# A hybrid decoder layer: the decay products of a group's heads in two blocks of four in place of four blocks of two

## The chip, the cores and the metric

One core of a Trainium2 chip runs the whole layer. The metric is the device time of one execution in microseconds (us), the median over runs.

The engines are named as the profile names them: PE is TensorE (PE for matmuls, PEld for its weight loads), DVE is VectorE, ACT is ScalarE, POOL is GpSimd, SP issues the loads of the weights.

## The reference

256 tokens go through one decoder layer of width 2048: a state-space branch and an attention branch in parallel, a gated merge, and a feed-forward part. The change lies in the state-space branch, which has 8 groups of 8 heads; all 256 positions are one chunk:

```
xbc = silu(causal_dwconv(xbc, conv_w, conv_b))          # after xbc, z = h @ w_in
a_cs = cumsum(dt * A)                                   # per head
decay = exp(where(causal, a_cs[l] - a_cs[s], -inf))     # per head, 256 x 256
cb = einsum('bclgn,bcsgn->bclsg', C, B)                 # per group
y_diag = einsum('bclsg,bclsgr,bcsgrp->bclgrp', cb, decay, x * dt)
y = y_diag + x * d_skip
yg = rmsnorm_per_group(y * silu(z)) * norm_w
```

The result is multiplied by `w_ssm_out`. All arithmetic is to be accurate to single precision.

## The kernel before

**Weights.** The kernel streams every weight matrix once, in pieces of 128 x 2048 (`unit`). A piece comes in two chunks. Each chunk of 128 x 1024 is split into a rounded part `whi` (ACT, line 182) and a rest `wlo` (DVE, line 183), and PE multiplies it in 24 matmuls: 16 with `whi` (lines 214 and 215), then 8 with `wlo` (line 217). `whi` and `wlo` have three buffers each, so that a chunk's split can begin when PE is done with the chunk three before it. One piece is called a unit here.

**The state-space branch.** Step g of a loop runs the ten units of group g (`group_units`, numbered 0 to 9). Units 4 to 9 are each followed by a causal convolution: one instruction of ACT (line 752), then three of DVE (line 755). Then, in steps 1 to 7, come four more units (gates or parts of the output product); step 8 has only such units.

**The core of a group** (`core_steps`) is spread over the units of the next step. It is a list of steps, and after each unit `sp.tick()` emits the next one. For group 7 the list is one shorter and is given 10 ticks, so the first three ticks take two steps each. An empty list is a tick without work. The steps that matter here, for a pair p of heads (four pairs in a group):

- `dec(p)` makes the decay times `cb` for two heads: on ACT lines 820 to 823, on DVE line 824, then a copy `mhl` in two parts, line 828 on ACT and 829 on DVE. `mhl` has two buffers.
- `ydot(p)` is four matmuls on PE (lines 839 and 840, twice each), from `mhl` into two tiles `cc`, of which there are four. DVE then adds them up with six instructions on 64 partitions each: lines 842, 844 and 845 for either head. After pairs 1 and 3 a product with the gate follows (line 847).
- `norm1` starts the norm of the group with two squares on ACT (lines 852 and 853).

The four matmuls of a `ydot` stand on PE between the last matmul of one unit and the first of the next; such a run of lines 839 and 840 is called a block.

**Order.** On PE the order is that of the code. On DVE and ACT a scheduler sets the order of the instructions when the kernel is built, from its own costs; on the chip each engine then takes its instructions in that order.

Of the kernel before, what the change touches and what calls it, by code (L numbers as in the profile page):

```python
# [160 lines left out]
def _body(tc, nc, d, out):  # L161
# [45 lines left out]
    def c_tile():  # L207
        return psum.tile([128, 512], F32, name="cc", bufs=4)
# [46 lines left out]
    def sm(name, i=0, n=1, rows=slice(0, 128)):  # L255
        o, _ = _SMALL[name]
        return small[rows, o + i:o + i + n]
# [403 lines left out]
    for o in range(KT):  # L661
# [8 lines left out]
        g = gl.pop(o)  # L670
# [88 lines left out]
    def core_steps(g):  # L759
        pr = pre[g % 2]  # L760
        st = {}
        steps = []
# [25 lines left out]
        def xtr(s):  # L788
            def f():
                ps = c_tile()  # L790
                for i in range(4):
                    PE.transpose(ps[:, i * 128:(i + 1) * 128], pr[:, 4 + i, s * 128:(s + 1) * 128], ident)  # L792
                xf = sd.tile([128, 8, 64], F32, name="xf", bufs=2)
                dtc = acol[:, s, 64 + 8 * g:72 + 8 * g]
                V.tensor_tensor(xf, ps.rearrange("p (h c) -> p h c", c=64),
                                dtc[:, :, None].to_broadcast([128, 8, 64]), op=MUL)
                xff = xf.rearrange("p (a b) c -> p a b c", b=2)
                hi, lo = st["x"][:, s, :, 0:4:3], st["x"][:, s, :, 1:3]
                S.activation(hi, xff, AF.Copy)
                V.tensor_tensor(lo, xff, hi.bitcast(F32), op=SUB)  # L800
            return f

        def load_a(p):
            ab = sd.tile([128, 2, T], F32, name="ab", bufs=2)
            h0 = 8 * g + 2 * p
            nc.gpsimd.dma_start(ab, bass.AP(tensor=acs.tensor, offset=acs.offset + h0 * T,
                                            ap=[[0, 128], [T, 2], [1, T]]))
            st["ab", p] = ab

        def dec(p):  # L810
            def f():
                if p == 0:
                    load_a(0)
                if p < 3:
                    load_a(p + 1)
                ab = st.pop(("ab", p))
                h0 = 8 * g + 2 * p
                m = sd.tile([128, 2, 384], F32, name="m", bufs=2)
                for h in range(2):
                    S.activation(m[:, h, 0:256], ab[:, h], AF.Relu, scale=-1.0, bias=acol[:, 0, h0 + h:h0 + h + 1])  # L820
                    S.activation(m[:, h, 256:384], ab[:, h, 128:256], AF.Relu, scale=-1.0,
                                 bias=acol[:, 1, h0 + h:h0 + h + 1])
                S.activation(m, m, AF.Exp, scale=-1.0)
                V.tensor_tensor(m, m, st["cb"][:, None].to_broadcast([128, 2, 384]), op=MUL)
                if g == 0 and p == 0:
                    sd.tile([128, 16], F32, name="pad2")
                mhl = sd.tile([128, 2, 2, 384], F32R, name="mhl", bufs=2)
                S.activation(mhl[:, 0], m, AF.Copy)
                V.tensor_tensor(mhl[:, 1], m, mhl[:, 0].bitcast(F32), op=SUB)
                st["m", p] = mhl  # L830
            return f

        def ydot(p):
            def f():
                m = st.pop(("m", p))
                for h in range(2):
                    ps = c_tile().rearrange("p (a t) -> p a t", t=T)
                    x0, x1 = [st["x"][:, s, p, 2 * h:2 * h + 2].rearrange("p a c -> p (a c)") for s in range(2)]
                    PE.matmul(ps, x0, m[:, :, h, 0:256], start=True, stop=False)  # L839
                    PE.matmul(ps[:, :, 128:], x1, m[:, :, h, 256:384], start=False, stop=True)  # L840
                    rs, ls = slice(h * 64, (h + 1) * 64), slice(64 - h * 64, 128 - h * 64)
                    V.scalar_tensor_tensor(yz[rs, p], pr[rs, 4 + p], sm("ssm_d", 4 * g + p, 1, rs), ps[rs, 0],
                                           op0=MUL, op1=ADD)
                    V.tensor_tensor(yz[rs, p], ps[rs, 1], yz[rs, p], op=ADD)
                    V.tensor_tensor(yz[rs, p], ps[ls, 0], yz[rs, p], op=ADD)
                if p % 2:
                    V.tensor_tensor(yz[:, p - 1:p + 1], yz[:, p - 1:p + 1], pr[:, p - 1:p + 1], op=MUL)
            return f
# [15 lines left out]
        def norm2():  # L864
            r = st["r"]
            for i in range(4):
# [4 lines left out]
            S.activation(yh, yz, AF.Copy)  # L871
            V.tensor_tensor(yt[:, b, 1, o:o + 4], yz, yh.bitcast(F32), op=SUB)

        steps = [[dt_cols, silu] if g == 0 else silu, [xtr(0), xtr(1), bc], dec(0), dec(1), ydot(0), dec(2), ydot(1), dec(3), ydot(2), [ydot(3), norm1],
                 [], [], norm1b, norm2]

        if g == G - 1:
# [33 lines left out]
    for step in range(9):  # L911
        if step < 8:
            for i in group_units(step):
                sp.tick()
        outs = [(((step - 3) // 2), ((step - 3) % 2) * 4 + u) for u in range(4)] if step >= 3 else []
        ng = {1: 4, 2: 4, 8: 8}.get(step, 0)
        for _ in range(ng):
            gate_ssm(go)
            go += 1
            sp.tick()  # L920
        for q, u in outs:
            out_unit(q, u, acc_done(q))
            sp.tick()
        sp.flush()
        if step < 8:
            nu = 14
            if step == 7:
                nu = 10
            sp.add(core_steps(step), nu)
# [140 lines left out]
```

## Time and profile before

| | |
|---|---|
| median of 3 runs | 2020.08 us (2019.61 to 2021.86) |
| the profiled execution | 2020.08 us, its span 2018.3 us |
| PE busy | 2012.8 us (100% of the span), 17203 matmuls |
| DVE, ACT, POOL busy | 1496.2, 1189.3, 79.0 us (74%, 59%, 4%) |
| granted clock of TensorE | 1.0 of full speed in the mean |
| DMA | 402.40 MB, mean 199 GB/s |

The span is the time from the first to the last instruction of the core; 1.8 us of the execution lie outside. A busy share is a mean over the whole span. The trace gives start and duration of each instruction; matmuls overlap, so what one costs is read from the distance between two starts.

### The profile page before, as it was taken

The page shows a single profiled execution, that of the slowest core. Times are in us where ns is not written, and L with a number is a line of the kernel's source. Part 1 is how long each engine was busy: PE and PEld are TensorE (multiplying, and loading weights), DVE is VectorE, ACT ScalarE, POOL GpSimd, SP SyncE. Part 2 cuts the span into 40 slices and gives each one's busy share as a digit, 9 for nine tenths or more (in the row PEclk, how much of TensorE's full clock was granted, in tenths as well). Part 3 has the DMA queues.
Part 4 walks back from the last instruction along what each step waited for, and adds up shares of the span by engine and source line. Part 5 has one row for each costly group of instructions (what it writes and reads, how often), then busy time and mean ns, then how long its engine had stood idle before and what let it go on. Part 6 is the DMA issues. An engine that isn't in the chain of part 4 may idle for free.

```text
span 2018.3 us, 40758 instructions
## 1 busy us (share of the span) xinstructions
PE 2012.8 (100%) x17203; PEld 1988.8 (99%) x17203; DVE 1496.2 (74%) x2206; ACT 1189.3 (59%) x1640; POOL 79.0 (4%) x100
## 2 busy tenths in 40 slices
PE   9999999999999999999999999999999999999999
PEld 7999999999999999999999999999999999999999
DVE  7588877656788798888989886677777765677554
ACT  6466655544768867667677645565555553455333
POOL 0012210000000000000000000000000000000000
PEclk9999999999999999999999999999999999999999
DMA  7555555656556556555565575555555555555555
GB/s 290 188 182 182 181 182 205 234 204 213 185 193 220 202 201 209 193 193 193 195 209 178 196 274 202 191 190 196 200 189 190 201 195 188 194 201 190 190 185 169
DMA packets 64351, 402.40 MB, mean 199 GB/s; under 512 B 7655, under 2 KB 10264, under 8 KB 20648
## 3 DMA queue, kind: packets, MB, share of 16 engines
q1 hardware_dynamic: 55384, 376.56, 52.8%
q0 software_dynamic: 5760, 18.97, 3.1%
q10 hardware_dynamic: 3024, 4.27, 0.6%
q8 instruction: 134, 2.20, 0.4%
q14 instruction: 49, 0.40, 0.1%
HBM read 394.44 MB, written 5.33 MB: 198 GB/s over the span
## 4 chain that ended last, share of the span: by engine, by line
PE 99%; DVE 0%; DMA 0%; issue 0%; SPq 0%; ACT 0%; DVEq 0%
PE mm L214 31%; PE mm L215 31%; PE mm L217 31%; PE mm L381 1%; PE mm L375 1%; PE mm L376 1%; PE cc L839 1%; PE cc L840 0%; PE cc L792 0%; DMA wraw<-wv 0%; PE cc L227 0%; PE cc L228 0%; PE cc L229 0%; PE cc L560 0%; DVE wlo L183 0%; DVE xt L317 0%
## 5 line engine op out<-in xcount | busy, mean ns | idle before, releaser
L182 ACT ACTIVATE whi<-wraw 128x1024 fp32r<-128x1024 f32 (+1 forms) x712 | 744.5, 1050 | 665.5 <-PE mm L215 584.3
L183 DVE TENSOR_TENSOR wlo<-wraw,whi 128x1024 fp32r<-128x1024 f32 (+1 forms) x712 | 864.2, 1218 | 242.5 <-ACT whi L182 237.3
L214 PE MATMUL mm<-hn,whi 128*128 128x256 f32 x1536 | 358.7, 277 | 0.0
L215 PE MATMUL mm<-hn,whi 128*128 128x256 f32 x1536 | 358.3, 277 | 0.0
L214 PE MATMUL mm<-fh,whi 128*128 128x256 f32 x1408 | 328.0, 276 | 0.0
L215 PE MATMUL mm<-fh,whi 128*128 128x256 f32 x1408 | 327.9, 277 | 0.0
L214 PEld LDWEIGHTS mm<-hn,whi 128*128 128x128 f32 x1536 | 288.5, 188 | 1.5 <-ACT whi L182 0.2
L215 PEld LDWEIGHTS mm<-hn,whi 128*128 128x128 f32 x1536 | 288.6, 188 | 0.1
L215 PEld LDWEIGHTS mm<-fh,whi 128*128 128x128 f32 x1408 | 264.5, 188 | 0.0
L214 PEld LDWEIGHTS mm<-fh,whi 128*128 128x128 f32 x1408 | 264.4, 188 | 0.0
L217 PE MATMUL mm<-hn,wlo 128*128 128x256 f32 x1536 | 205.6, 277 | 0.0
L217 PEld LDWEIGHTS mm<-hn,wlo 128*128 128x128 f32 x1536 | 188.4, 188 | 0.0
L217 PE MATMUL mm<-fh,wlo 128*128 128x256 f32 x1408 | 188.4, 277 | 0.0
L214 PE MATMUL mm<-hp,whi 128*128 128x256 f32 x768 | 180.1, 278 | 0.0
L215 PE MATMUL mm<-hp,whi 128*128 128x256 f32 x768 | 179.2, 277 | 0.0
L217 PEld LDWEIGHTS mm<-fh,wlo 128*128 128x128 f32 x1408 | 172.6, 188 | 0.0
L214 PE MATMUL mm<-a,whi 128*128 128x256 f32 x704 | 164.4, 276 | 0.0
L215 PE MATMUL mm<-a,whi 128*128 128x256 f32 x704 | 164.4, 277 | 0.0
L214 PEld LDWEIGHTS mm<-hp,whi 128*128 128x128 f32 x768 | 144.4, 188 | 0.1
L215 PEld LDWEIGHTS mm<-hp,whi 128*128 128x128 f32 x768 | 144.3, 188 | 0.1
L215 PEld LDWEIGHTS mm<-a,whi 128*128 128x128 f32 x704 | 132.3, 188 | 0.0
L214 PEld LDWEIGHTS mm<-a,whi 128*128 128x128 f32 x704 | 132.2, 188 | 0.0
(308 smaller groups left out, 3242.0 us busy)
## 6 DMA issues: line engine op xcount, KB each, us to landing
wraw<-wup SPq DMA_DIRECT2D x88, 1024.0 KB, 4.8
wraw<-wssd SPq DMA_DIRECT2D x80, 1024.0 KB, 4.9
wraw<-wqk SPq DMA_DIRECT2D x32, 1024.0 KB, 4.8
wraw<-wso SPq DMA_DIRECT2D x32, 1024.0 KB, 4.8
wraw<-wd SPq DMA_DIRECT2D x32, 1024.0 KB, 4.8
wraw<-wga SPq DMA_DIRECT2D x16, 1024.0 KB, 4.9
wraw<-wao SPq DMA_DIRECT2D x16, 1024.0 KB, 5.0
wraw<-wgs SPq DMA_DIRECT2D x16, 1024.0 KB, 4.8
```

Of the source, the lines that this page charges most:

```text
L182: last_hi[0] = S.activation(hi[:, :n // 2], raw[:, s], AF.Copy)
L183: V.tensor_tensor(lo[:, :n // 2], raw[:, s], hi[:, :n // 2].bitcast(F32), op=SUB)
L214: PE.matmul(ps, w, xh[:, k0 + k], start=first and k == 0, stop=False)
L215: PE.matmul(ps, w, xl[:, k0 + k], start=False, stop=False)
L217: PE.matmul(ps, lo[:, k * 128:(k + 1) * 128], xh[:, k0 + k], start=False, stop=last and k == nk - 1)
L375: PE.matmul(pst[tt], hph[:, k0 + k, ts], wh, start=first and k == 0, stop=False)
L376: PE.matmul(pst[tt], hpl[:, k0 + k, ts], wh, start=False, stop=False)
L381: PE.matmul(pst[tt], hph[:, k0 + k, ts], wl, start=False, stop=last and k == 1)
L839: PE.matmul(ps, x0, m[:, :, h, 0:256], start=True, stop=False)
```

## The change

Only the list of steps changes. Two `ydot` come together after one tick, so that PE has two blocks of eight matmuls per group in place of four blocks of four; `dec(2)` and `dec(3)` follow the first of these blocks. The list keeps its length of 14.

```
-        steps = [[dt_cols, silu] if g == 0 else silu, [xtr(0), xtr(1), bc], dec(0), dec(1), ydot(0), dec(2), ydot(1), dec(3), ydot(2), [ydot(3), norm1],
+        steps = [[dt_cols, silu] if g == 0 else silu, [xtr(0), xtr(1), bc], dec(0), dec(1), [], [ydot(0), ydot(1)], dec(2), dec(3), [],
+                 [ydot(2), ydot(3), norm1],
                  [], [], norm1b, norm2]
```

For groups 0 to 6 the blocks stood after units 4, 6, 8 and 9; now they stand after units 5 and 9. On PE, one block of before, of group 2, with the last matmuls ahead of it and the first behind it:

```order
L217 MATMUL mm<-hn,wlo 128x256 x8
L839 MATMUL cc<-mhl,xx 128x512
L840 MATMUL cc<-mhl,xx 128x2x128
L839 MATMUL cc<-mhl,xx 128x512
L840 MATMUL cc<-mhl,xx 128x2x128
L214 MATMUL mm<-hn,whi 128x256
```

And the first block of the same group now:

```order
L217 MATMUL mm<-hn,wlo 128x256 x8
L839 MATMUL cc<-mhl,xx 128x512
L840 MATMUL cc<-mhl,xx 128x2x128
L839 MATMUL cc<-mhl,xx 128x512
L840 MATMUL cc<-mhl,xx 128x2x128
L839 MATMUL cc<-mhl,xx 128x512
L840 MATMUL cc<-mhl,xx 128x2x128
L839 MATMUL cc<-mhl,xx 128x512
L840 MATMUL cc<-mhl,xx 128x2x128
L214 MATMUL mm<-hn,whi 128x256
```

The second block has moved up behind the first; what stood between them, two units, now stands ahead of and behind the two. On DVE, behind a block in group 2 (`slotA` and `pre_5560` hold the group's results and the outputs of the convolutions), before:

```order
L845 TENSOR_TENSOR slotA<-cc,slotA 64x256
L842 SCALAR_TENSOR_TENSOR slotA<-slotA,small,cc 64x256
L829 TENSOR_TENSOR mhl<-m,mhl 128x768
L844 TENSOR_TENSOR slotA<-cc,slotA 64x256
L183 TENSOR_TENSOR wlo<-wraw,whi 128x1024
L845 TENSOR_TENSOR slotA<-cc,slotA 64x256
L755 SCALAR_TENSOR_TENSOR pre_5560<-mm,small,pre_5560 128x255
L183 TENSOR_TENSOR wlo<-wraw,whi 128x1024
```

And behind the first block now:

```order
L845 TENSOR_TENSOR slotA<-cc,slotA 64x256
L842 SCALAR_TENSOR_TENSOR slotA<-slotA,small,cc 64x256 x2
L844 TENSOR_TENSOR slotA<-cc,slotA 64x256 x2
L845 TENSOR_TENSOR slotA<-cc,slotA 64x256 x2
L842 SCALAR_TENSOR_TENSOR slotA<-slotA,small,cc 64x256
L829 TENSOR_TENSOR mhl<-m,mhl 128x768
L844 TENSOR_TENSOR slotA<-cc,slotA 64x256
L755 SCALAR_TENSOR_TENSOR pre_5560<-mm,small,pre_5560 128x255
L845 TENSOR_TENSOR slotA<-cc,slotA 64x256
L755 SCALAR_TENSOR_TENSOR pre_5560<-mm,small,pre_5560 128x254
L847 TENSOR_TENSOR slotA<-slotA 128x512
L755 SCALAR_TENSOR_TENSOR pre_5560<-mm,small,pre_5560 128x253
```

In both, the rows ahead of these are the same six (lines 755, 842, 755, 844, 755 and 845, the first one shown), and ahead of them stands a `wlo`. Behind the twelve rows the next `wlo` follows. So between two `wlo` there stood nine instructions and now there are twenty, and the three convolution instructions of the next unit are among them. The order is the same in groups 0 to 6.

## Rows read from the trace of the kernel before

**Rows 1.** Page, busy time of the engines over the whole span.

```profile
PE 2012.8 (100%) x17203; PEld 1988.8 (99%) x17203; DVE 1496.2 (74%) x2206; ACT 1189.3 (59%) x1640; POOL 79.0 (4%) x100
```

**Rows 2.** Windows: stretch of all blocks; its length, then each engine's busy time.

```profile
535.00:1145.00 610.00, 610.00 (x5294) 606.48 (x5293) 528.77 (x777) 436.34 (x607) 19.92 (x37) 1.00 0.57 198
```

**Rows 3.** Instructions on tile cc: count, duration in ns, first and last start.

```profile
L839 PE MATMUL cc<-mhl,xx x64: 397/399/399, 558.1 to 1138.3; 128*128 128x512 f32 x64
```

**Rows 4.** Timeline of PE, group 3's second block: start, us, what.

```profile
812.76 0.40 PE L839 MATMUL cc<-mhl,xx 128*128 128x512 f32 x1
...
813.47 0.28 PE L214 MATMUL mm<-hn,whi 128*128 128x256 f32 x1
...
815.30 1.07 PE L217 MATMUL mm<-hn,wlo 128*128 128x256 f32 x8
...
823.46 1.07 PE L217 MATMUL mm<-hn,wlo 128*128 128x256 f32 x8
```

**Rows 5.** Timeline of DVE, the same stretch; idle time ahead in brackets.

```profile
813.14 1.23 DVE L183 TENSOR_TENSOR wlo<-wraw,whi 128x1024 fp32r<-128x1024 f32 x1 [0.68 <-ACT whi L182]
814.29 0.48 DVE L755 SCALAR_TENSOR_TENSOR slotA<-mm,small,slotA 128x255 f32<-128x255 f32 x1
...
815.79 0.47 DVE L755 SCALAR_TENSOR_TENSOR slotA<-mm,small,slotA 128x253 f32<-128x253 f32 x1
816.29 0.43 DVE L845 TENSOR_TENSOR slotA<-cc,slotA 64x256 f32<-64x256 f32 x1
816.75 0.49 DVE L842 SCALAR_TENSOR_TENSOR slotA<-pre,small,cc 64x256 f32<-64x256 f32 x1
817.26 0.96 DVE L829 TENSOR_TENSOR mhl<-m,mhl 128x768 fp32r<-128x768 f32 x1
818.25 0.43 DVE L844 TENSOR_TENSOR slotA<-cc,slotA 64x256 f32<-64x256 f32 x1
818.71 1.23 DVE L183 TENSOR_TENSOR wlo<-wraw,whi 128x1024 fp32r<-128x1024 f32 x1
819.97 0.42 DVE L845 TENSOR_TENSOR slotA<-cc,slotA 64x256 f32<-64x256 f32 x1
820.42 0.48 DVE L755 SCALAR_TENSOR_TENSOR slotA<-mm,small,slotA 128x255 f32<-128x255 f32 x1
820.82 0.68 DVE L847 TENSOR_TENSOR slotA<-slotA,pre 128x512 f32<-128x512 f32 x1
821.42 0.48 DVE L755 SCALAR_TENSOR_TENSOR slotA<-mm,small,slotA 128x254 f32<-128x254 f32 x1
821.81 1.22 DVE L183 TENSOR_TENSOR wlo<-wraw,whi 128x1024 fp32r<-128x1024 f32 x1
```

**Rows 6.** Timeline of PE, start of group 7's first block.

```profile
1114.01 0.40 PE L839 MATMUL cc<-mhl,xx 128*128 128x512 f32 x1
```

**Rows 7.** Timeline of DVE behind that block.

```profile
1116.58 0.98 DVE L842 SCALAR_TENSOR_TENSOR slotA<-pre,small,cc 64x256 f32<-64x256 f32 x2
1117.60 0.88 DVE L844 TENSOR_TENSOR slotA<-cc,slotA 64x256 f32<-64x256 f32 x2
1118.50 0.87 DVE L845 TENSOR_TENSOR slotA<-cc,slotA 64x256 f32<-64x256 f32 x2
1119.41 0.96 DVE L829 TENSOR_TENSOR mhl<-m,mhl 128x768 fp32r<-128x768 f32 x1
```

**Rows 8.** Timeline of DVE in the first stage, one row.

```profile
36.37 1.22 DVE L183 TENSOR_TENSOR wlo<-wraw,whi 128x1024 fp32r<-128x1024 f32 x1
```

**Rows 9.** Timeline of PE in the first stage; idle time ahead in brackets.

```profile
31.69 1.08 PE L381 MATMUL mm<-wlo,hp 128*128 128x512 f32 x4
32.61 0.39 PE L375 MATMUL mm<-whi,hp 128*128 128x512 f32 x1
...
37.65 1.21 PE L381 MATMUL mm<-wlo,hp 128*128 128x512 f32 x4 [0.29 <-DVE wlo L183]
38.69 0.39 PE L375 MATMUL mm<-whi,hp 128*128 128x512 f32 x1
```

## The prediction

> **What bounds the kernel now.** I read the page first: PE is busy 2012.8 us of a span of 2018.3 [rows 1]. Then the windows, for the stretch that holds all blocks: PE is busy 610.00 of 610.00 us there, at a granted clock of 1.00, DVE 528.77 (87%) and ACT 436.34 (72%) [rows 2]. So PE never waits in this stage, and two things can move the time: fewer nanoseconds on PE itself, or a wait on PE that isn't there now. The timelines of PE and DVE around one block then tell how far each split of a weight chunk is ahead of PE. The reader is to see there that DVE takes its instructions in a fixed order, so that a `wlo` that could start must stand behind whatever the scheduler put ahead of it.
>
> **What it removes from PE.** 64 matmuls of line 839 [rows 3], two in a block, make 32 blocks; now there are 16. The matmuls stay the same in number and shape. In a block of four the next unit starts 813.47 - 812.76 = 0.71 us after the block's start. From there to the first `wlo` matmul it takes 815.30 - 813.47 = 1.83 us; an undisturbed chunk takes (823.46 - 815.30)/3 = 2.72, of which 16 of 24 matmuls are 1.81 [rows 4]. So a change between blocks and units costs about 0.02 us beside the matmuls themselves, and 16 of these are 0.3 us. That is all that merging can save.
>
> [...]
>
> **What it adds on DVE.** The split of chunk n needs a buffer that PE gives back three chunks earlier, and `whi` of the chunk first. So when a block starts, at T, the `wlo` of the third chunk behind it is just being made: in group 3 the block starts at 812.76 [rows 4], that `wlo` at 813.14 (it waited for `whi`), and the pile of small instructions behind it at 814.29, which is T + 1.53 [rows 5]. The next `wlo`, for the fourth chunk, is what the change delays. Before, it stands behind nine instructions: it starts at 818.71 and ends at 819.94 [rows 5], and PE's matmuls with it start at 823.46 [rows 4]. It is 3.5 us ahead.
>
> In the changed kernel the first block of groups 0 to 6 has the same geometry, with a pile of twenty instructions ahead of the fourth `wlo`. From start to start, by the timeline of DVE unless another group is named [rows 5]:
>
> - the six that alternate between convolution and first head, up to the next line 842: 816.75 - 814.29 = 2.46
> - then lines 842, 844 and 845, twice each, alternating between the two halves of the partitions. This stands in group 7 of before: 1119.41 - 1116.58 = 2.83 [rows 7]
> - the last head's 842 (817.26 - 816.75 = 0.51), `mhl` of line 829 (0.99), line 844 (0.46): 1.96
> - line 755 ahead of an 845 (816.29 - 815.79 = 0.50), 845 (0.45), 755 (0.40), 847 (0.60), 755 (0.39): 2.34. These convolution instructions belong to unit 6, which ends on PE at T + 1.44 + 5.44 = T + 6.88; DVE comes to them at T + 8.78, so they don't wait.
>
> The fourth `wlo` starts at T + 1.53 + 2.46 + 2.83 + 1.96 + 2.34 = T + 11.12 and takes 1.22 [rows 5]: T + 12.34. PE needs it at 823.46 - 812.76 = 10.70 behind the block's start, and 0.71 later since the block is twice as long: T + 11.41 [rows 4]. It comes 0.93 us late, and PE has no other work to take in its place.
>
> What such a wait costs can be read in the first stage, where PE waited for a `wlo` behind some additions on DVE: it ended at 36.37 + 1.22 = 37.59 [rows 8], the matmuls started at 37.65, and the four took 38.69 - 37.65 = 1.04 up to the next, against 32.61 - 31.69 = 0.92 without a wait [rows 9]. So 0.06 and 0.12 come on top, and one wait costs 0.93 + 0.18 = 1.11 us. In seven groups: 7.8 us.
>
> **What is late next.** Behind the late `wlo` stand another `mhl` and the fifth `wlo`: start at T + 11.12, 1.15 (814.29 - 813.14) to the `mhl`, 0.99, 1.22: T + 14.48. PE, which now runs late itself, wants it at T + 12.40 + 1.04 + 1.81 = T + 15.25. It is 0.8 us ahead, and there are three more chunks for DVE to catch up in before the second block. That block isn't delayed: its last `mhl` is there at about T + 13.3, and it starts eight chunks behind the first one, at T + 23.
>
> Behind the second block the fourth `wlo` has only the first three parts ahead, without `mhl`: 1.53 + 2.46 + 2.83 + 0.51 + 1.22 = 8.55 against 11.41, so 2.9 us ahead. In group 7 no convolution follows. There line 842 starts later, 1116.58 - 1114.01 = 2.57 behind the block's start [rows 6, 7]; two runs of 2.83, `mhl` (0.99) and 847 (0.60) follow, and the `wlo` ends at 2.57 + 5.66 + 1.59 + 1.22 = 11.04, still 0.4 us ahead. I count no wait for it. On ACT two copies of line 828 now stand together, but it has 28% of idle time in this stage [rows 2], and the `whi` next to them isn't wanted for several us; I cost it at nothing. If that cover were gone, a late `whi` would delay the same `wlo`, and its price is the upper bound below.
>
> **The sum.** The profiled execution takes 2020.08 us, 1.8 of it outside its span, and is also the median of the runs. 2020.08 + 7.8 - 0.3 = 2027.6 us.
>
> **Bounds.** The term that no row shows as it will stand is the pile of twenty. From below: if the six on opposite halves stood 0.39 apart, the shortest distance in these rows (821.81 - 821.42), they would take 2.34 in place of 2.83, and if the third `wlo` started with the block, where its buffer comes free, in place of 0.38 us behind it (813.14 - 812.76) [rows 4, 5], the pile would start at T + 1.15. With both, 0.06 of the 0.93 is left, a wait costs 0.24, and the sum is 2021.5; with the first alone 0.62 and 2024.1. From above: if the pile started as late as in group 7, 2.57 in place of 1.53, each wait would cost 1.97 + 0.18 = 2.15, and the sum would be 2034.8. I take the middle values, since the very sequence of the six and the very start of 1.53 stand in rows of this kernel.
>
> **The rivals.**
>
> - *No wait: the fourth `wlo` is in time.* It needs the pile to be 0.93 us shorter than worked out, for instance because DVE, idle for 13% of the stage [rows 2], starts on it earlier. For it: the margin is small beside a pile of 9.6 us. Against it: the pile can't start before its `wlo`, which waits for `whi`, and that for PE; the 0.68 us of idle time ahead of it [rows 5] show that. Then only the 0.3 us are left: 2019.8, no change. This is the case on the other side; it decides from the point at which the wait is under 0.6 - 0.18 us per group, since 7 x 0.6 is 0.2% of the time.
> - *Half a wait*, between the two: DVE is faster in the pile, or at it sooner, as in the lower bounds. 2021.5 to 2024.1.
> - *More waits*: the last group's `wlo`, only 0.4 us ahead, is late too, or the pile starts late in all groups because ACT comes late with `whi`. 2030.5 to 2035.
> - *A gain above 0.3 us* has no place in the rows: PE waits for nothing here now [rows 2].
>
> **How the numbers follow.** The waits as worked out: 0.64, with an own range of 2025.0 to 2029.8 (a third of a microsecond either way in each of seven groups). No wait: 0.18. Half a wait: 0.10. More waits: 0.08. The likeliest gives 2027.6. To leave out no more than 2 in 10 the range has to reach down to the case of no wait, 2019.6, and ends at 2029.8. A change below 0.2%, or 4.0 us, can't be told from none here. Slower by more: the waits as worked out and more waits, 0.72, and a small part of half a wait, 0.03: 0.75. Within 0.2%: no wait and most of half a wait, 0.23. Faster: 0.02, for what I haven't seen.
>
> **What would show it.** In the list of waits a new row must stand, PE line 217 on DVE's `wlo`, line 183, about seven times, some 0.9 us each, all of them four chunks behind the first block of a group. PE's busy time in the stretch of the blocks would fall short of its length for the first time. DVE's timeline behind a first block must show the next `wlo` starting about 11.1 us behind the block's start. The blocks themselves must take 1.44 us with what lies beside them. I am wrong if PE is busy without a break there, if the `wlo` starts well ahead of 10 us, or if PE waits for another instruction, as the `whi` of ACT or an `mhl` ahead of a block.

## The result, and the profile after

The changed kernel takes 2031.09 us in the median of six executions, against 2019.87 for the kernel before in the same runs. The ratio is 1.0055 (95%: 1.0044 to 1.0065), so it is slower by about 11 us. The prediction was 2027.6, with a range that ended at 2029.8: the direction was right, and the time lies above the range.

The six times fall into two groups: 2027.9, 2028.32 and 2028.33, and then 2033.86, 2034.23 and 2034.71. The median lies in the gap between them, where no execution is. So there are two things to explain: what lifts all six to 2028, and what adds 6 us to three of them. The profiled execution is one of the longer three (2033.86 us, its span 2032.1).

The page of the changed kernel has this row; it answers to [rows 1]:

```profile
PE 2020.5 (99%) x17203; PEld 1995.7 (98%) x17203; DVE 1497.9 (74%) x2206; ACT 1190.9 (59%) x1640; POOL 79.0 (4%) x100
```

PE has the same 17203 matmuls, but is busy 7.7 us longer than before (2012.8 there). Idle time can't do this, since a PE that stands still isn't busy. The other half of the increase of the span, 13.8 us, is idle time, as the list of PE's waits shows (line waited for, us in total, how often, the longest):

```profile
PE mm L217 <- DVE wlo L183: 6.0, 7, 1.0
PE cc L269 <- DVE onesr L262: 1.1, 1, 1.1
PE mm L375 <- ACT whi L197: 0.6, 1, 0.6
PE cc L286 <- DVE nsp L281: 0.4, 1, 0.4
PE mm L381 <- DVE wlo L183: 0.3, 1, 0.3
```

Two of these rows come from the change: the first, seven waits for `wlo`, and that of line 286, which is one matmul in the norm of the last group. The kernel before has neither.

**The seven waits.** PE's timeline behind the first block of group 3 (start, duration, engine, line, operation, tiles; idle time before it in brackets):

```profile
809.13 0.40 PE L839 MATMUL cc<-mhl,xx 128*128 128x512 f32 x1
...
810.54 0.29 PE L214 MATMUL mm<-hn,whi 128*128 128x256 f32 x1
...
817.82 1.07 PE L217 MATMUL mm<-hn,wlo 128*128 128x256 f32 x8
...
821.54 1.19 PE L217 MATMUL mm<-hn,wlo 128*128 128x256 f32 x8 [0.84 <-DVE wlo L183]
822.57 0.28 PE L214 MATMUL mm<-hn,whi 128*128 128x256 f32 x1
```

And DVE's timeline in the same stretch:

```profile
809.51 1.23 DVE L183 TENSOR_TENSOR wlo<-wraw,whi 128x1024 fp32r<-128x1024 f32 x1 [1.49 <-ACT whi L182]
810.66 0.48 DVE L755 SCALAR_TENSOR_TENSOR slotA<-mm,small,slotA 128x255 f32<-128x255 f32 x1
...
813.12 0.99 DVE L842 SCALAR_TENSOR_TENSOR slotA<-pre,small,cc 64x256 f32<-64x256 f32 x2
...
815.96 0.49 DVE L842 SCALAR_TENSOR_TENSOR slotA<-pre,small,cc 64x256 f32<-64x256 f32 x1
...
817.92 0.48 DVE L755 SCALAR_TENSOR_TENSOR slotA<-mm,small,slotA 128x255 f32<-128x255 f32 x1
...
820.27 1.22 DVE L183 TENSOR_TENSOR wlo<-wraw,whi 128x1024 fp32r<-128x1024 f32 x1
821.41 0.95 DVE L829 TENSOR_TENSOR mhl<-m,mhl 128x768 fp32r<-128x768 f32 x1
822.28 1.22 DVE L183 TENSOR_TENSOR wlo<-wraw,whi 128x1024 fp32r<-128x1024 f32 x1
```

With T = 809.13 the pile starts at T + 1.53 and its four parts take 2.46, 2.84, 1.96 and 2.35 us. The fourth `wlo` starts at T + 11.14 and ends at 821.49. PE starts 0.05 us later. It would have started one undisturbed chunk of 2.72 us [rows 4] behind 817.82, at 820.54. So PE is held up for 1.00 us. Then these eight matmuls take 822.57 - 821.54 = 1.03 us up to the next one, where eight take 8/24 x 2.72 = 0.91 without a wait; the 0.12 more is called the restart here. Together the wait costs 1.12 us, 0.28 more than the 0.84 in its bracket, because the profile lets the last matmul ahead of a wait stay busy for 0.28 us when the next could start 0.11 us behind it. The list has 6.0 us for the seven waits, so they cost 6.0 + 7 x 0.28 = 8.0 us; the 2.0 of it that aren't idle stand in PE's busy time.

**The wait at line 286.** In group 7 the norm's sum of squares (line 281 on DVE) feeds a matmul of 512 columns (line 286 on PE). First the changed kernel, DVE and then PE:

```profile
1152.79 0.68 DVE L847 TENSOR_TENSOR slotA<-slotA,pre 128x512 f32<-128x512 f32 x1
...
1154.53 0.68 DVE L854 TENSOR_TENSOR sqt<-sqt,sqt 128x512 f32<-128x512 f32 x1
1155.24 0.42 DVE L855 TENSOR_TENSOR sqt<-sqt 128x256 f32<-128x256 f32 x1
1155.59 1.22 DVE L183 TENSOR_TENSOR wlo<-wraw,whi 128x1024 fp32r<-128x1024 f32 x1
1156.72 0.42 DVE L281 TENSOR_TENSOR nsp<-sqt,nsp 128x256 fp32r<-128x256 f32 x1
```

```profile
1155.86 1.07 PE L217 MATMUL mm<-yt,wlo 128*128 128x256 f32 x8
1157.29 0.47 PE L286 MATMUL cc<-nsp,onesr 128*128 128x512 f32 x1 [0.35 <-DVE nsp L281]
1157.59 0.28 PE L214 MATMUL mm<-yt,whi 128*128 128x256 f32 x1
```

The kernel before at the same place, again DVE and PE:

```profile
1148.45 0.42 DVE L281 TENSOR_TENSOR nsp<-sqt,nsp 128x256 fp32r<-128x256 f32 x1
```

```profile
1149.58 0.39 PE L286 MATMUL cc<-nsp,onesr 128*128 128x512 f32 x1
1149.81 0.28 PE L214 MATMUL mm<-yt,whi 128*128 128x256 f32 x1
```

Before, line 281 ended at 1148.87, 0.7 us ahead of PE. Now twelve additions of two pairs stand behind the last block where there were six of one pair, then the product with the gate (847) and the whole chain of the norm, and line 281 ends at 1157.14. The eight matmuls of line 217 that start at 1155.86 are over 8 x 0.113 = 0.91 us later, at 1156.77; line 286 starts at 1157.29, 0.52 late, and the step to the next matmul is 0.30 where it was 0.23. Together this wait costs 0.59 us.

**The 6 us that no wait shows.** The windows give busy time and, in brackets, the number of instructions of PE, PEld, DVE, ACT and POOL, then the granted clock, the DMA share and GB/s. Behind line 286, first the kernel before and then the changed one:

```profile
1160.00:1300.00 140.00, 140.00 (x1238) 140.00 (x1237) 101.13 (x135) 73.56 (x94) 4.84 (x9) 1.00 0.64 226
```

```profile
535.00:1145.00 610.00, 603.98 (x5229) 599.54 (x5228) 521.71 (x761) 434.44 (x603) 19.93 (x37) 1.00 0.57 196
1160.00:1300.00 140.00, 140.00 (x1191) 140.00 (x1191) 99.35 (x132) 73.83 (x93) 4.84 (x9) 1.00 0.62 218
```

From 1160 to 1300 us PE is busy 140.00 of 140.00 us, at a granted clock of 1.00, in both kernels. Only the number of matmuls tells them apart: 1238 before, 1191 now. The same matmuls start 140/1191 = 117.5 ns apart where it was 113.1. (A window also counts the matmuls that reach over its edges; from start to start the two are 117.8 and 113.3 ns, the latter 2.72/24 by [rows 4].) Start by start this wide spacing begins behind the wait at line 286 and holds until the next matmul that isn't part of a weight product, at 1315.89; such a matmul is called foreign below. These are 158.3 us for 56 chunks of 24 matmuls, which take 56 x 2.72 = 152.3 us otherwise: 6 us are lost. That is the distance between the two groups of times. Below, *narrow* and *wide* stand for these two spacings.

### The profile page after: what moved, and what is told of

Its sections match the earlier page's. It is cut to its first block, busy times and chain, and to the rows that moved or that the text cites. A ratio compares the mean times of both kernels' runs of the same rounds, so it can differ in the third digit from the quotient of the medians.

```text
span 2032.1 us, 40754 instructions
## 1 busy us (share of the span) xinstructions
PE 2020.5 (99%) x17203; PEld 1995.7 (98%) x17203; DVE 1497.9 (74%) x2206; ACT 1190.9 (59%) x1640; POOL 79.0 (4%) x100
## 4 chain that ended last, share of the span: by engine, by line
PE 94%; DVE 5%; issue 0%; ACT 0%; DMA 0%; SPq 0%; DVEq 0%
PE mm L217 29%; PE mm L215 29%; PE mm L214 29%; PE mm L381 1%; PE mm L375 1%; PE mm L376 1%; DVE wlo L183 1%; DVE slotA L842 1%; DVE slotA L845 1%; DVE slotA L844 1%; DVE pre L755 1%; PE cc L839 0%; DVE slotA L755 0%; PE cc L792 0%; DVE mhl L829 0%
```

## The experiments

The first question was which groups cost what. Experiments 1 and 2 divide the change between groups 0 to 6 and group 7.

**1. The change in groups 0 to 6 alone (e1_g7_before).**

```
+        if g == G - 1:
+            steps = [[dt_cols, silu] if g == 0 else silu, [xtr(0), xtr(1), bc], dec(0), dec(1), ydot(0), dec(2), ydot(1), dec(3), ydot(2), [ydot(3), norm1],
+                 [], [], norm1b, norm2]
```

> The change in groups 0 to 6, the old list of steps in group 7. Theory A (seven waits of PE for wlo behind the first blocks cost 1.12 us each; the rest of the loss comes from the last group, where PE waits 0.35 us for the split sum of squares of the norm and then, in some executions, goes on at 117.8 ns per matmul in place of 113.4 until the next foreign matmul): 2019.9 + 7.8 - 0.3, about 2027.5 us in every execution, no cluster 6 us higher, seven waits in the list and none of line 286. Rival B (the long slow stretch belongs to the merged blocks wherever they stand, or to the chip's state in those executions): two clusters again, near 2027.5 and 2033.5.

Measured: 2027.76 us, ratio 1.0038 (1.0025 to 1.0050), five executions from 2026.82 to 2030.3. The seven waits are there (5.9 us in total), the one at line 286 isn't, and no execution reached 2033. So the 7 us common to all executions come from groups 0 to 6. The wide spacing doesn't belong to group 7 alone, though: in this profile it stands behind the second of the seven waits, for the 12 us up to the next block (see experiment 5).

**2. The change in group 7 alone (e2_g7_only).** The reverse edit: the old list everywhere, the new one for `g == G - 1`.

> The old list in groups 0 to 6, the change in group 7 alone. Theory A: no wait for wlo; one wait at line 286 of 0.35 us, 0.6 with its restart; executions fall into two clusters, near 2020.4 us and, where the slow pitch takes hold, near 2026.4. Rival B (slow pitch has to do with groups 0 to 6, or with the seven waits): one cluster, 2019.9 to 2020.5.

Measured: 2021.17 us, ratio 1.0005 (0.9996 to 1.0013). There is no wait for line 183 in the stage of the groups and one of 0.4 us at line 286. Ten of eleven executions lie between 2020.1 and 2022.14, the eleventh at 2026.17, about 5 us above the others. The profiled one is among the ten.

**3. Blocks of eight, but DVE's sums of the second pair three ticks later (e3_late_sums).** `ydot` is split into its matmuls and its sums; group 7 has the old list. Here and below the diff shows the changed part of the list.

```
-  [], [ydot(0), ydot(1)], dec(2), dec(3), [], [ydot(2), ydot(3), norm1],
+  [], [ymm(0), ymm(1), ysum(0)], dec(2), dec(3), ysum(1),
+  [ydot(2), ydot(3), norm1],
```

> Groups 0 to 6 keep the two blocks of eight matmuls, but DVE's six sums of the second pair in the first block come three ticks later, so that the next wlo again stands behind nine instructions; group 7 has the old list. Theory A: no wait of PE, about 2019.6 us, the same as before; the blocks themselves cost or save no more than 0.3 us. Rival C (the merged blocks cost on PE itself, or through the tiles cc that they hold): still about 2027 us, or PE busy short of the stretch's length.

Measured: 2019.46 us, ratio 0.9996 (0.9987 to 1.0005). Its window over the stage:

```profile
535.00:1145.00 610.00, 610.00 (x5300) 606.76 (x5299) 530.32 (x777) 436.75 (x607) 19.96 (x37) 1.00 0.57 198
```

And DVE's timeline behind the block that starts at 805.69 (here the sums are lines 865, 867 and 868):

```profile
807.21 0.48 DVE L755 SCALAR_TENSOR_TENSOR slotA<-mm,small,slotA 128x255 f32<-128x255 f32 x1
...
811.19 0.43 DVE L867 TENSOR_TENSOR slotA<-cc,slotA 64x256 f32<-64x256 f32 x1
811.65 1.23 DVE L183 TENSOR_TENSOR wlo<-wraw,whi 128x1024 fp32r<-128x1024 f32 x1
```

The pile starts at the same T + 1.52, but the fourth `wlo` at T + 5.96 in place of T + 11.14, and PE is busy 610.00 of 610.00. So the block of eight on PE costs nothing: what made PE wait were the eleven additional instructions on DVE ahead of that `wlo`, which came with the sums of the second pair. The window has 5300 matmuls where the kernel before has 5294 [rows 2], 6 more at 610/5300 = 0.115 us: 0.7 us saved, too little for the interval. Not all of it is merging. The kernel before holds a short wait in group 1 that neither its list of waits nor its busy time shows; ACT first, then PE:

```profile
678.75 0.41 ACT L280 ACTIVATE nsp<-sqt 128x256 fp32r<-128x256 f32 x1
679.06 1.05 ACT L182 ACTIVATE whi<-wraw 128x1024 fp32r<-128x1024 f32 x1
```

```profile
679.10 1.07 PE L217 MATMUL mm<-hn,wlo 128*128 128x256 f32 x8
680.16 0.39 PE L214 MATMUL mm<-hn,whi 128*128 128x256 f32 x1
680.39 0.28 PE L215 MATMUL mm<-hn,whi 128*128 128x256 f32 x1
```

Line 214 starts 0.05 us behind the end of that `whi`, 1.06 us behind the start of the eight matmuls in place of 0.91, and the next step is 0.23 in place of 0.11: 0.27 us in all. In experiment 3 ACT makes this `whi` ahead of line 280, and the same two steps are 0.91 and 0.11. That leaves 0.4 us for 14 mergings, 0.03 each.

**4. The changed kernel with a foreign matmul ahead of each of eight units (e4_breaker).** Ahead of each of eight units behind the last group, PE gets one more matmul of 512 columns, whose result isn't used:

```
+        warm_up(1)
         out_unit(3, u, merge)
```

> The changed kernel with one idle matmul of 512 columns put ahead of each of the last eight units of the output product, in the stretch that ran at 117.8 ns. Each costs some 0.25 us, 2 us together. Theory A: a foreign matmul ends the slow pitch, so no execution keeps it past the first of them: all near 2028.2 + 2 = 2030 us, at most 1 us more where the slow pitch held up to there. Rival D (the slow pitch is a state of the chip that lasts some 160 us whatever runs): two clusters, near 2030 and 2036.

Measured: 2029.92 us, ratio 1.0047 (1.0034 to 1.0059), and all five executions from 2029.56 to 2030.69, one group. At 0.23 us each, the step behind line 286 in the kernel before, the eight added matmuls cost 1.8 us, which puts the lower group of 2027.1 to 2028.4 at 2028.9 to 2030.2. This agrees with foreign matmuls ending a wide spacing, but five executions without a long one could also be chance. Experiment 8 was made for that.

**5. The changed kernel unaltered, once more (e5_again).**

> The changed kernel once more, nothing altered, for the two clusters (2028.2 and 2034.2 us in the first six executions). Theory A: the same two clusters, and a profile that tells which one it is of: seven waits for wlo in either, the long stretch at 117.8 ns per matmul behind the wait of line 286 only where the execution is near 2034. Rival E (the higher cluster is longer waits, not a slower pitch): in a profile near 2034 the waits are longer than in one near 2028.

Measured: 2027.64 us, ratio 1.0036 (1.0024 to 1.0049); all five between 2027.14 and 2028.44. This time the profile is of an execution in the lower group. Its windows:

```profile
535.00:1145.00 610.00, 604.08 (x5234) 599.67 (x5233) 521.99 (x761) 434.94 (x602) 19.92 (x37) 1.00 0.56 196
1160.00:1300.00 140.00, 140.00 (x1238) 140.00 (x1237) 102.68 (x138) 76.58 (x96) 4.84 (x9) 1.00 0.65 226
```

And PE at line 286:

```profile
1157.85 0.48 PE L286 MATMUL cc<-nsp,onesr 128*128 128x512 f32 x1 [0.36 <-DVE nsp L281]
1158.16 0.28 PE L214 MATMUL mm<-yt,whi 128*128 128x256 f32 x1
```

The same wait (0.36 against 0.35 us) is there, but behind it PE is back at the narrow spacing at once: 1238 matmuls from 1160 to 1300, as before. So the same kernel with the same wait may or may not get the wide spacing, and no other difference of that size between the two profiles was found. Over both sets, 8 of 11 executions lie at 2027.1 to 2028.4 and 3 at 2033.9 to 2034.7. The seven waits, 5.9 us in the list here, cost 5.9 + 7 x 0.28 = 7.9 us, 1.13 each.

The wide spacing isn't tied to line 286 either. Behind the wait for `wlo` in group 4, the long execution of the changed kernel and this one differ in the same way:

```profile
905.00:915.00 10.00, 10.00 (x87) 10.00 (x87) 8.87 (x12) 3.98 (x5) 0.00 (x0) 1.00 0.83 309
905.00:915.00 10.00, 10.00 (x91) 10.00 (x90) 9.49 (x13) 4.89 (x6) 0.00 (x0) 1.00 0.86 309
```

In the long one it lasts from 903.76 to the second block of the group, at 915.89, and costs 0.5 us. Six profiles have the seven waits; in five of them the wide spacing stands behind one or two (six of 42 waits in all), in this one behind none, and each time the next block ends it. So a wait of either kind can be followed by it. In the stage of the groups a block comes within 12 us; behind line 286 nothing foreign comes for 158, and only there does it cost 6 us.

**6. Only the first two blocks merged (e6_first_pair).**

```
-  [], [ydot(0), ydot(1)], dec(2), dec(3), [], [ydot(2), ydot(3), norm1],
+  [], [ydot(0), ydot(1)], dec(2), dec(3), ydot(2), [ydot(3), norm1],
```

> Only the first two blocks of each group are merged; the third and fourth stay apart, as before. Theory A: the seven waits for wlo stay, each 1.1 us; the sums of the last pair stand as before in the last group, so no wait at line 286 and no higher cluster: 2027.6 us. Rival F (the loss comes from the second block, with the norm behind it): 2020.

Measured: 2027.49 us, ratio 1.0036 (1.0022 to 1.0050), 2027.26 to 2029.01. The seven waits (5.9 us) are there, line 286 doesn't wait.

**7. Only the last two blocks merged (e7_second_pair).**

```
-  [], [ydot(0), ydot(1)], dec(2), dec(3), [], [ydot(2), ydot(3), norm1],
+  ydot(0), dec(2), ydot(1), dec(3), [], [ydot(2), ydot(3), norm1],
```

> Only the third and fourth blocks are merged. Theory A: no wait for wlo, since the one behind the second block was worked out to be 2.9 us ahead; the wait of line 286 in the last group stays, 0.35 us: 2020.4 us, and some executions near 2026.4 with the slow pitch. Rival F: 2027 or more.

Measured: 2019.98 us, ratio 1.0001 (0.9992 to 1.0009). No wait in the stage, PE is busy 610.00 of 610.00 us; line 286 waits 0.4 us. Ten of eleven executions lie between 2019.29 and 2021.10, the eleventh at 2027.45, 7.5 us above their middle. Six and seven together show that the first block of a group makes the seven waits, and the second block of the last group the wait at line 286.

**8. One foreign matmul, behind the last of the eight units (e8_one_breaker).**

```
     for u in range(8):
         out_unit(3, u, merge)
+    warm_up(1)
```

> The changed kernel with one idle matmul of 512 columns behind the last unit of the output product, 22 chunks after the wait of line 286 and 34 ahead of the next foreign matmul. Theory A: a slow pitch that takes hold at the wait ends there: it costs 22 x 24 x 4.45 ns = 2.3 us in place of 6.0, so two clusters at 2028.5 and 2030.8 us, none at 2034. Rival D (it lasts its time whatever runs): 2028.5 and 2034.5.

Measured: 2028.19 us, ratio 1.0042 (1.0030 to 1.0055). Three executions lie at 2027.38 to 2028.19, two at 2030.6 and 2030.86: the upper group is there again, but some 3 us above the lower in place of 6. The profile is of the one at 2030.6. PE at the added matmul, line 269:

```profile
1219.95 0.39 PE L269 MATMUL cc<-onesr 128*128 128x512 f32 x1
1220.18 0.28 PE L214 MATMUL mm<-mt,whi 128*128 128x256 f32 x1
```

And its windows ahead of this matmul and behind it:

```profile
1160.00:1215.00 55.00, 55.00 (x470) 55.00 (x468) 43.97 (x56) 29.86 (x34) 4.85 (x9) 1.00 0.76 265
1225.00:1300.00 75.00, 75.00 (x664) 75.00 (x664) 48.38 (x70) 41.13 (x56) 0.00 (x0) 1.00 0.56 197
```

The same stretches in the changed kernel's long execution:

```profile
1160.00:1215.00 55.00, 55.00 (x469) 55.00 (x469) 44.00 (x56) 29.69 (x34) 4.84 (x9) 1.00 0.76 265
1225.00:1300.00 75.00, 75.00 (x640) 75.00 (x639) 46.31 (x66) 39.43 (x54) 0.00 (x0) 1.00 0.53 186
```

Up to the added matmul both are wide (470 and 469 matmuls in 55 us); behind it one has 664 in 75 us and the other 640. One foreign matmul of 0.23 us ends the wide spacing. It lasted 62 us in place of 158, which is 22 chunks in place of 56: 2.4 us in place of 6. The rest of the 3 us between the groups is within the spread of the executions; in the profiled one, PE also waits 1.2 us for the `whi` of line 197, against 0.6 in experiment 5.

## Why the prediction was wrong, point by point

**PE bounds the stage, and any wait shows at once: right, but for one wait.** In the stage of the groups PE stands still for 6.02 us (603.98 of 610.00), all of it in the seven waits. That "PE never waits in this stage" before was read from a busy time of 610.00; the 0.27 us in group 1 (experiment 3) don't show in it, and they are gone in the changed kernel.

**The pile on DVE and the seven waits: right in place, cause and size.** The `wlo` was predicted to start at T + 11.12 and starts at T + 11.14, with each of the four parts within 0.01 us of its term. The estimate of a wait, 0.93 + 0.18 = 1.11, was measured at 1.12 in group 3; the sum of 7.8 at 7.9 to 8.0. The `wlo` behind it is not late, as worked out, and PE waits for no `mhl` and no `whi`. Taking the second pair's sums away from that place (experiment 3) took the waits away.

**The saving of 0.3 us by merging: about right.** It is some 0.4 us: 0.03 for each merging where the prediction had 0.02. The block of eight takes 810.54 - 809.13 = 1.41 us, the 1.42 of two blocks of four less 0.01; the rest lies in the first matmuls of the units behind the blocks. The 0.27 us of the wait in group 1 that goes away with the old order come on top. The sum had no term for it, and that it goes is luck, not part of the mechanism.

**"In group 7 ... I count no wait for it": the step that failed.** It was said of the `wlo` behind the first block of group 7, and there it holds: PE doesn't wait for it. But behind the second block of that group, of which the prediction says nothing, twelve sums stand ahead of something else on DVE, the norm, whose line 281 was 0.7 us ahead of PE before and is now behind it. The prediction followed one consumer of the late engine and left out the other. By the rows this wait costs 0.59 us. With it the sum is 2020.08 + 7.9 + 0.6 - 0.4 - 0.3 = 2027.9; the lower group of times, 2027.1 to 2028.4 over eight of eleven executions, is there.

**The price of a wait, its length and 0.18 us: right for the seven but for a short wide stretch behind some, wrong for this one in some executions.** Behind line 286 PE can take up the wide spacing and keep it for 158 us, 6 us in all. That is 3 of the 6 executions behind the result, enough to put the median at 2031.09, outside the range. The same kernel in experiment 5 had none in five, and its median of 2027.64 lies inside: how many executions take it up is chance as far as is known, but that some can was left out. No row of [rows 1 to 9] has a price like that, though the trace of the kernel before holds a short stretch of it (the last section). Shown by the runs: that the upper group is this spacing (the windows of a long and a short execution of the same kernel, 1191 and 1238 matmuls at the same busy time), and that a foreign matmul ends it (experiment 8). For the two single long executions of experiments 2 and 7 it was only argued, since no profile is of them. In their favour, both kernels have the wait at line 286, and none of the 42 executions of the kernel before and of the 21 of experiments 1, 3 and 6, all without that wait, lies 4 us above its kernel's median.

**The rivals.** *No wait* and *half a wait* are out by the seven waits. *More waits* named about the right time, 2030.5 to 2035, but for a late `wlo` or `whi`, and neither is late. Its time doesn't make it right: the missing 6 us aren't a wait at all.

**What stays open.** What makes PE take up the wide spacing in one execution and not in another, after waits of 0.35 and 0.36 us, wasn't found. A kernel that gives line 281 its 0.7 us again inside the full change wasn't run; experiment 1, which drops the merging in group 7, and experiment 6, which drops the second merging in every group, have neither the wait nor the long times, and experiment 3 (blocks of eight without any wait) isn't measurably faster than the kernel before.

## What to carry to other kernels

When work is moved together on an engine that runs close behind the bounding one, walk every consumer of that engine from the place on, not only the nearest stream: here the weights' `wlo` and the norm both stood behind the same sums, and a lead of 0.7 us was spent. Price a wait on a saturated PE from start to start, or by the number of matmuls in windows that hold the same work, in several executions: busy share and granted clock show nothing when only the spacing changes, and a busy time without a break can hide a wait of 0.15 us. And when a set of times falls into two groups, compare a profile of each before explaining the median.

## What the runs showed of the hardware

- **Two spacings of the same matmuls.** Matmuls of 256 columns start 113.3 ns or 117.8 ns apart (113.1 and 117.5 by windows of 1238 and 1191 matmuls in 140 us), with PE busy 100% and a granted clock of 1.00 in both.
- **What ends the wide one.** A single matmul of 512 columns that isn't of the stream, 0.23 us long, brought PE back to the narrow spacing (470 in 55 us ahead of it, 664 in 75 us behind it). Without it the wide spacing held for 158 us.
- **It needs no wait to begin.** In the kernel before, the two chunks between two attention blocks, 48 matmuls from 328.70 to 334.36 us, are 5.66/48 = 0.118 us apart, and the first starts 0.12 us behind the last matmul of a block, without a wait; the next block ended it.

```profile
328.58 0.28 PE L563 MATMUL cc<-pt,vt 128*128 128x256 f32 x1
328.70 0.28 PE L214 MATMUL mm<-hp,whi 128*128 128x256 f32 x1
...
334.36 0.40 PE L560 MATMUL cc<-pt,vt 128*128 128x512 f32 x1
```
